# A hybrid encoder layer on one core: the first head group's inverse roots reach all partitions through memory in place of through the PE

## The chip, the cores and the metric

The kernel runs on one core of one Trainium2 chip. The metric is device time in microseconds (us) for one execution; the figure before the change is the median of three runs. Five engines run side by side, each in the order of its own queue: PE (matrix products and transposes), DVE (vector), ACT (scalar functions and copies), POOL, and SP, which here only issues transfers (DMAs). They wait for each other through semaphores. Results of PE land in PSUM, everything else that is worked on lies in on-chip memory with 128 partitions; "memory" below is the chip's DRAM.

## The reference, cut to what matters

One encoder layer over 1024 tokens of 1024 features. One projection feeds two token mixers: group A (windowed attention, 8 heads of 64) and group B (neighbourhood attention on a grid, 8 heads of 64). Each group's output, 512 features wide, is normalised by itself before the two go through one output projection. Then come a gated MLP with a convolution and a last normalisation.

```python
def rmsnorm(x, g):
    xf = x.astype(jnp.float32)
    y = xf * lax.rsqrt(jnp.mean(xf * xf, axis=-1, keepdims=True) + EPS)
    return (y * g.astype(jnp.float32)).astype(x.dtype)
...
        o_a = window_gqa_sink(qa, ka, va, sink[l])
        o_b = neighbourhood_attention(qb, kb, vb, rpb[l])
        mix = jnp.concatenate([rmsnorm(o_a, norm_a[l]), rmsnorm(o_b, norm_b[l])], axis=-1)
        h = h + jnp.einsum('bse,ed->bsd', mix, w_out[l])
...
```

The change concerns `rmsnorm(o_a, norm_a[l])` alone: for each of the 1024 tokens one number, 1/sqrt(mean square + eps), by which the 512 features of group A are multiplied.

## The kernel before

**Layout.** Activations lie transposed: features on the partitions, tokens along a row. Group A's output is four tiles `mix[0]` to `mix[3]`, each 128 features by 1024 tokens. The sum of squares over features is thus a sum over partitions and tiles, and the number that comes out for each token is needed on all 128 partitions, since every feature is multiplied by it.

**Stages.** The attention stage runs from about 50 us (its first scores start at 53.6) to about 350 us (its last product with the values at 348.5). In it two streams are interleaved: attention units (scores, softmax, transposes of the weights, products with the values) and, as filler between them, blocks of projection products (`rest`, L778). The filler's jobs are the projections of 15 column tiles (`Project`, jobs 0 to 14) and the output projection's group A part (`OutA`, jobs 15 to 22). A job has 16 steps, eight to each half of the tokens, of three matmuls each. A table `aux` hangs single pieces of work on a step: `aux[12, 5]` runs after step 5 of job 12. After the attention come the output projection and the MLP, in which PE works on one long row of products.

**What sets the order.** PE's instructions stand in the order in which the code issues them (`manual_schedule`, L136). DVE, ACT, POOL and SP are ordered by a scheduler from that stream; `tc.high_priority` (L827) lets a piece of work stand earlier than its place. Every engine then works strictly in its order: an instruction whose inputs are not there holds all that stand behind it on that engine.

**Group A's norm.** Five pieces hang in `aux` (L835). `square_a` squares and adds the four tiles to one tile `norm["sq"]` of 128 by 1024, four adds to a half. `narrow_a`, called for each half, transposes that tile in blocks of 128 tokens into PSUM and lets DVE sum each row; the second call takes the square root (ACT) and the reciprocal (DVE) of all eight columns at once. `norm["v"]` then holds, on partition p and in column c, the inverse root of token 128c + p. `wide_a(h)` spreads four columns: `widen` (L231) transposes each column, broadcast to 128 by 128, against the identity, so that all 128 output partitions get the row of 128 tokens; ACT copies the bank of 512 tokens to one half of the tile `rstda`. `wide_a(0)` hangs on step 11 and `wide_a(1)` on step 13 of job 12. The eight products `normed_a` (L831), one to a tile and half on DVE, hang on job 13; job 14, the last projection, splits the normalised tiles into two parts for the output projection.

**Beside it** on the same engines: DVE subtracts the rounded part of each block of transposed attention weights (`pl`, L430), without which PE's second product with the values (L541) cannot run; it adds the bias to the scores and takes the row minimum (L415); it takes scores of the next job's projection out of PSUM (L246). SP loads the projection's weights (`raw`, L163) and rearranges queries and keys between partitions (L304 to L307). It also loads a strip of biases for each of group B's heads (`rr`, L485): 128 rows of 489 numbers, one to a partition, that overlap and lie within 961 numbers of memory (the rows of a 16 by 8 pattern with steps of 31 and 1).

Of the kernel before, what the change touches and what calls it, by code (L numbers as in the profile page):

```python
# [13 lines left out]
F32 = mybir.dt.float32  # L14
F32R = mybir.dt.float32r
AF = mybir.ActivationFunctionType
# [3 lines left out]
D, S, HD = 1024, 1024, 64  # L20
# [37 lines left out]
def hybrid_layer(tc, xT, w_first, w_in, w_out, w_gate, w_up, w_down, small, sink, rpb, consts, rope, out):  # L58
    nc = tc.nc
    with ExitStack() as ctx:  # L60
# [7 lines left out]
        tpool = inner("temps", 3)  # L68
        apool = inner("att", 2)
        spool = inner("stats", 6)  # L70

        slots = {"xg": 16, "op": 14, "mix": 8, "rstd": 1}

        def big(name, tag, dt=F32):
            return lpool.tile([128, S], dt, name=name, tag=tag, bufs=slots[tag])
# [4 lines left out]
        def bank(name, tag):  # L80
            return psum.tile([128, HALF], F32, name=name, tag=tag)

        f32 = lambda ap: ap.bitcast(F32)
        tsl = lambda h: slice(h * HALF, (h + 1) * HALF)
# [48 lines left out]
        ident = cst[:, K_ID:K_ID + 128]  # L133
# [76 lines left out]
        def inverse_narrow(sqs, dim, tag, n=4):  # L210

            ps = bank("ss", tag)
            v = cpool.tile([128, n], F32, name="v4", tag="v4", bufs=4, padded_shape=[128, 4])
            if len(sqs) == 1:
                for c in range(n):
                    nc.tensor.transpose(ps[:, c * 128:(c + 1) * 128], sqs[0][:, c * 128:(c + 1) * 128], ident)
                with tc.high_priority(offset=500):
                    nc.vector.tensor_reduce(v, ps[:, 0:n * 128].rearrange("p (c w) -> p c w", w=128), axis=mybir.AxisListType.X, op=ALU.add)
                    nc.scalar.activation(v, v, AF.Sqrt, bias=eps, scale=1.0 / dim)
            else:  # L220
                for i, sq in enumerate(sqs):
                    for c in range(n):
                        nc.tensor.matmul(ps[:, c:c + 1], sq[:, c * 128:(c + 1) * 128], ones[:, 0:1], start=c == 0 and i == 0,
                                         stop=i == len(sqs) - 1, skip_group_check=True)
                with tc.high_priority(offset=500):
                    nc.scalar.activation(v[:, 0:n], ps[:, 0:n], AF.Sqrt, bias=eps, scale=float(D) / dim)
            with tc.high_priority(offset=500):
                nc.vector.reciprocal(v[:, 0:n], v[:, 0:n])
            return v

        def widen(v, tag, n=4):  # L231

            wide = bank("sw", tag)
            for c in range(n):
                nc.tensor.transpose(wide[:, c * 128:(c + 1) * 128], v[:, c:c + 1].to_broadcast([128, 128]), ident)
            return wide
# [327 lines left out]
        mg, h1, norm = [None] * 8, [None] * KT, {"halves": 0}  # L564
# [187 lines left out]
        live = {"op": 0}  # L752
# [23 lines left out]
        aux = {}  # L776
# [42 lines left out]
                if h == 1:  # L819
                    inverse_root(norm["v"], 512)  # L820

        def wide_a(h):
            def go():
                if h == 0:
                    live["op"] += 1
                    norm["a"] = big("rstda", "op")
                with tc.high_priority(offset=500):  # L827
                    nc.scalar.activation(norm["a"][:, tsl(h)], widen(norm["v"][:, 4 * h:4 * h + 4], "pj"), AF.Copy)
            return go

        def normed_a(i, h):  # L831
            return lambda: nc.vector.scalar_tensor_tensor(
                mix[i][:, tsl(h)], mix[i][:, tsl(h)], col(C_NA + i), norm["a"][:, tsl(h)], op0=ALU.mult, op1=ALU.mult)

        aux[11, 8], aux[12, 2], aux[12, 5], aux[12, 11], aux[12, 13] = square_a, narrow_a, narrow_a, wide_a(0), wide_a(1)  # L835
        for i in range(8):
            aux[13, 1 + i + i // 2] = normed_a(*divmod(i, 2))
        filler = rest()
# [241 lines left out]
        for h in range(2):  # L1080
            for d in range(KT):
                if h == 0 and d + 2 < KT:
                    wo.append(load_wo(d + 2, False))
                ps = bank("pj", ("o", "s", "pj")[(h * KT + d) % 3])
# [4 lines left out]
                if h == 1 and d == 1:  # L1089
                    v = inverse_narrow([total[0]], D, "pt")  # L1090
# [157 lines left out]
        v = inverse_narrow([total[1]], D, "pt")  # L1248
# [196 lines left out]
        sq, todo, vs = {}, [], {}  # L1445
# [59 lines left out]
        for i, (p, j, c) in enumerate(order):  # L1505
# [10 lines left out]
            ps = banks[p, j]  # L1516
# [26 lines left out]
        for k, cols in enumerate(quarters):  # L1543
            for j in (2, 3):
                ps = banks[6, j]
# [111 lines left out]
```

## Time and profile before

| | |
|---|---|
| median of 3 runs | 1020.83 us (1020.73 to 1021.33) |
| the profiled execution's own time | 1020.98 us |
| its span, first to last instruction | 1019.2 us |
| instructions | 14884 |
| busy: DVE | 834.7 us (82%) |
| busy: ACT | 561.6 us (55%) |
| busy: POOL | 108.6 us (11%) |
| granted clock of PE, mean | 0.998 |

The profiled execution is one more run of the kernel; times of single instructions come from it, counted from the start of its span. Work outside the span, 1.8 us of its own time, is not in the trace. Busy time is a share of the span; a matmul's end is modelled and matmuls overlap, so the start of one and the start of the next tell its price better than its length does. In a row of the timeline stand the start, the time to the end, the engine, the source line, the operation, what is written and read, and how many instructions were put together; in brackets how long the engine had been idle before and what ended that.

### The profile page before, as it was taken

What the parts mean: (1) busy time and instruction counts of PE and PEld (TensorE: products, weight loads), DVE (VectorE), ACT (ScalarE), POOL (GpSimd) and SP (SyncE); (2) the same over time, 40 slices, a digit from 0 to 9 for tenths busy, and PEclk for the clock granted to TensorE, in tenths of its full rate; (3) what the DMA queues carried; (4) which work ended last, traced back from release to release, by engine and by line L of the source; (5) the groups of instructions that cost most, each with busy time, mean ns of one, the idle gap of its engine ahead of it and who ended that gap; (6) DMA issues with size and microseconds to landing.
All of it is one profiled execution on the core that took longest, in us unless ns stands there. A gap on an engine that the chain in (4) does not pass through costs nothing.

```text
span 1019.2 us, 14884 instructions
## 1 busy us (share of the span) xinstructions
PE 1008.2 (99%) x5094; PEld 889.9 (87%) x5094; DVE 834.7 (82%) x1570; ACT 561.6 (55%) x1081; POOL 108.6 (11%) x188
## 2 busy tenths in 40 slices
PE   9999999999999999999999999999999999999996
PEld 8888888999988888888888888888888888888886
DVE  7889888768898799999987786786777688986675
ACT  8567776657676554565544443444443645544451
POOL 0233333222252100000000000000000000000002
PEclk9999999999999999999999999999999999999999
DMA  8223122333335356222552333323232698866644
GB/s 293 78 78 94 32 72 63 83 83 83 83 87 161 101 179 237 84 87 79 186 180 99 114 114 114 104 94 118 100 132 82 231 343 317 299 226 235 221 156 166
DMA packets 68220, 144.94 MB, mean 142 GB/s; under 512 B 8240, under 2 KB 18736, under 8 KB 68144
## 3 DMA queue, kind: packets, MB, share of 16 engines
q1 hardware_dynamic: 58064, 118.82, 36.0%
q10 hardware_dynamic: 10080, 25.17, 6.4%
q8 instruction: 40, 0.66, 0.3%
q14 instruction: 36, 0.29, 0.1%
HBM read 103.58 MB, written 28.57 MB: 130 GB/s over the span
## 4 chain that ended last, share of the span: by engine, by line
PE 88%; DVE 5%; ACT 3%; issue 2%; DMA 1%; DVEq 0%; SPq 0%; ACTq 0%
PE x L1017 7%; PE x L1018 7%; PE x L1016 7%; PE dn L1018 7%; PE dn L1017 7%; PE dn L1016 7%; PE pj L178 6%; PE pj L180 6%; PE pj L179 6%; PE y L1017 4%; PE y L1018 4%; PE y L1016 4%; PE s L392 3%; PE z L1017 2%; PE z L1016 2%; PE z L1018 2%
## 5 line engine op out<-in xcount | busy, mean ns | idle before, releaser
L1016 PE MATMUL x<-hg,whi 128*128 128x512 f32 x352 | 133.5, 379 | 0.0
L1017 PE MATMUL x<-hg,whi 128*128 128x512 f32 x352 | 133.4, 379 | 0.0
L1018 PE MATMUL x<-hg,wlo 128*128 128x512 f32 x352 | 133.4, 379 | 0.0
L1016 PE MATMUL dn<-xd,whi 128*128 128x512 f32 (+1 forms) x330 | 120.8, 366 | 0.0
L1018 PE MATMUL dn<-xd,wlo 128*128 128x512 f32 (+1 forms) x330 | 120.6, 365 | 0.0
L1017 PE MATMUL dn<-xd,whi 128*128 128x512 f32 (+1 forms) x330 | 120.5, 365 | 0.0
L419 ACT ACTIVATE p<-p,nm 128x385 f32<-128x385 f32 (+3 forms) x128 | 75.0, 586 | 62.5 <-DVE nm L415 59.8
L990 ACT ACTIVATE whi<-ws 128x512 fp32r<-128x512 f32 (+1 forms) x100 | 60.7, 621 | 73.8 <-DVE ws L1126 14.7
L423 POOL TENSOR_SCALAR p<-p,sm 128x384 f32<-128x384 f32 (+1 forms) x128 | 79.8, 637 | 192.0 <-DVE sm L421 159.7
L178 PE MATMUL pj<-xgh,whi 128*128 128x512 f32 x245 | 99.7, 407 | 0.0
L179 PE MATMUL pj<-xgl,whi 128*128 128x512 f32 x245 | 93.0, 379 | 0.2 <-DVE xgl L654 0.2
L180 PE MATMUL pj<-xgh,wlo 128*128 128x512 f32 x245 | 92.9, 379 | 0.0
L990 ACT ACTIVATE whi<-raw 128x512 fp32r<-128x512 f32 (+1 forms) x102 | 60.9, 610 | 48.9 <-PE x L1017 17.3
L991 DVE TENSOR_TENSOR wlo<-ws,whi 128x512 fp32r<-128x512 f32 (+1 forms) x100 | 66.5, 679 | 19.1 <-ACT whi L990 18.8
L1477 POOL TENSOR_TENSOR h<-h,wide 128x256 f32<-128x256 f32 (+1 forms) x6 | 5.4, 916 | 670.3 <-ACT wide L1473 670.3
L430 DVE TENSOR_TENSOR pl<-pt,ph 128x384 fp32r<-128x384 f32 (+2 forms) x108 | 63.6, 589 | 15.6 <-ACT ph L429 13.7
L1016 PEld LDWEIGHTS x<-hg,whi 128*128 128x128 f32 x352 | 66.5, 189 | 9.5
L1018 PEld LDWEIGHTS x<-hg,wlo 128*128 128x128 f32 x352 | 66.5, 189 | 9.5
L1017 PEld LDWEIGHTS x<-hg,whi 128*128 128x128 f32 x352 | 66.5, 189 | 9.4
L991 DVE TENSOR_TENSOR wlo<-raw,whi 128x512 fp32r<-128x512 f32 (+1 forms) x102 | 66.5, 668 | 5.1 <-ACT whi L990 5.1
L1018 PEld LDWEIGHTS dn<-xd,wlo 128*128 128x128 f32 x330 | 62.5, 189 | 8.1 <-DVE wlo L991 0.4
L1347 ACT ACTIVATE xd<-xd 128x512 fp32r<-128x512 f32 x77 | 47.3, 625 | 40.2 <-DMA xd<-x 39.7
(267 smaller groups left out, 2515.2 us busy)
## 6 DMA issues: line engine op xcount, KB each, us to landing
xd<-x SPq DMA_DIRECT2D x77, 256.0 KB, 5.1
raw<-in_w_down_dram SPq DMA_DIRECT2D x72, 256.0 KB, 4.5
raw<-in_w_gate_dram SPq DMA_DIRECT2D x22, 512.0 KB, 3.4
raw<-in_w_up_dram SPq DMA_DIRECT2D x22, 512.0 KB, 3.5
x<-c ACTq DMA_DIRECT2D x22, 512.0 KB, 2.6
raw<-in_w_in_dram SPq DMA_DIRECT2D x30, 256.0 KB, 2.8
raw<-in_w_down_dram SPq DMA_DIRECT2D x36, 192.0 KB, 4.4
x<-t ACTq DMA_DIRECT2D x11, 512.0 KB, 2.6
```

The costliest lines, as they stand in the source:

```text
L178: nc.tensor.matmul(ps, w[0], mv(x[0][:, tsl(h)]), start=first, stop=False)
L179: nc.tensor.matmul(ps, w[0], mv(x[1][:, tsl(h)]), start=False, stop=False)
L180: nc.tensor.matmul(ps, w[1], mv(x[0][:, tsl(h)]), start=False, stop=last)
L419: nc.scalar.activation(p[:, j, 0:e], p[:, j, 0:e], AF.Exp, bias=nm, scale=-1.0, accum_out=sm[:, j:j + 1])
L423: nc.gpsimd.tensor_scalar(p[:, i, 0:m], p[:, i, 0:m], sm[:, i:i + 1], 1.0, op0=ALU.mult, op1=ALU.mult)
L430: mark["rest"] = nc.vector.tensor_tensor(pl[:, 0:n], ps[:, 0:n], f32(ph[:, 0:n]), op=ALU.subtract)
L990: nc.scalar.activation(hi, src, AF.Copy)
L991: nc.vector.tensor_tensor(lo, src, f32(hi[:, :, :]), op=ALU.subtract)
L1016: nc.tensor.matmul(ps, w[0], x[0], start=first and i == 0, stop=False, skip_group_check=True)
L1017: nc.tensor.matmul(ps, w[0], x[1], start=False, stop=False, skip_group_check=True)
L1018: nc.tensor.matmul(ps, w[1], x[0], start=False, stop=last and i == len(ws) - 1, skip_group_check=True)
L1347: nc.scalar.activation(hi, f32(lo), AF.Copy)
```

## The change

In place of `wide_a(0)` and `wide_a(1)` one piece, `wide_a`, hangs on step 9 of job 12. One transpose turns the 128 by 8 tile of inverse roots into 8 rows of 128 tokens in a PSUM bank. ACT copies them to the first eight partitions of `norm["sq"]`, whose sums of squares are no longer needed. SP writes the eight rows to a buffer `roots` in memory, 4 KB, and then reads that buffer, 1024 tokens in a row, once for each of the 128 partitions into the tile `rstda`. The eight products on DVE are the same and read the same tile; where they stand in DVE's order is set by the scheduler.

```diff
+        spread_pool = ctx.enter_context(tc.tile_pool(name="roots", bufs=1, space=bass.MemoryType.DRAM))
+        roots = spread_pool.tile([8, 128], F32, name="roots")
...
-        def wide_a(h):
-            def go():
-                if h == 0:
-                    live["op"] += 1
-                    norm["a"] = big("rstda", "op")
-                with tc.high_priority(offset=500):
-                    nc.scalar.activation(norm["a"][:, tsl(h)], widen(norm["v"][:, 4 * h:4 * h + 4], "pj"), AF.Copy)
-            return go
+        def wide_a():
+            live["op"] += 1
+            norm["a"] = big("rstda", "op")
+            ps, row = bank("row", "pj"), norm["sq"][0:8, 0:128]
+            nc.tensor.transpose(ps[0:8, 0:128], norm["v"], ident)
+            with tc.high_priority(offset=500):
+                nc.scalar.activation(row, ps[0:8, 0:128], AF.Copy)
+                nc.sync.dma_start(roots, row)
+                nc.sync.dma_start(norm["a"], bass.AP(tensor=roots.tensor, offset=roots.offset, ap=[[0, 128], [1, S]]))
...
-        aux[11, 8], aux[12, 2], aux[12, 5], aux[12, 11], aux[12, 13] = square_a, narrow_a, narrow_a, wide_a(0), wide_a(1)
+        aux[11, 8], aux[12, 2], aux[12, 5], aux[12, 9] = square_a, narrow_a, narrow_a, wide_a
```

Source lines of the changed kernel lie two to three higher. Three places of the engines' orders show what moves.

**SP, from the rearranging of one head's queries and keys on.** Before:

```order
L305 DMA q<-kb 64x1024
L307 DMA ka<-kb 64x1024
L306 DMA kb<-ka 64x1024
L163 DMA raw<-in_w_in_dram 128x512
L163 DMA raw<-in_w_out_dram 128x512
L485 DMA rr<-in_rpb_dram 128x1x489
```

and now:

```order
L307 DMA q<-kb 64x1024
L309 DMA ka<-kb 64x1024
L308 DMA kb<-ka 64x1024
L831 DMA roots<-sq 8x128
L165 DMA raw<-in_w_in_dram 128x512
L832 DMA rstda<-roots 128x1024
L165 DMA raw<-in_w_out_dram 128x512
L487 DMA rr<-in_rpb_dram 128x1x489
```

The write of the eight rows stands directly behind the last rearranging transfer, the read for all partitions one weight load later; the load of the output projection's first weights stands behind both.

**DVE, while job 12 ends.** `mixa` is group A's output, `rstda` the spread roots. Before, five of the eight products stood here:

```order
L430 TENSOR_TENSOR pl<-pt,ph 128x384
L832 TENSOR_SCALAR mixa<-mixa,par,rstda 128x512
L415 ISA p,nm<-s,xb 128x384
L415 ISA nm 128x1
L832 TENSOR_SCALAR mixa<-mixa,par,rstda 128x512 x4
L430 TENSOR_TENSOR pl<-pt,ph 128x384
L246 TENSOR_TENSOR t<-pj,rstd_334 128x8x8x8
```

and now none does:

```order
L432 TENSOR_TENSOR pl<-pt,ph 128x384
L417 ISA p,nm<-s,xb 128x384
L417 ISA nm 128x1
L432 TENSOR_TENSOR pl<-pt,ph 128x384
L248 TENSOR_TENSOR t<-pj,rstd_337 128x8x8x8
```

The five have gone further down; everything else keeps its place among itself.

**DVE, some ten instructions later, in job 13.** `v` are the values of a later pair of heads. Before, three products stood ahead of the second `pl` of 256 columns, and that `pl` stood ahead of the copy of job 13's first half out of PSUM (L246):

```order
L421 RECIPROCAL sm<-sm 128x2
L832 TENSOR_SCALAR mixa<-mixa,par,rstda 128x512
L430 TENSOR_TENSOR pl<-pt,ph 128x384
L415 ISA p,nm<-s,xb 128x384
L415 ISA nm 128x1
L832 TENSOR_SCALAR mixa<-mixa,par,rstda 128x512 x2
L334 TENSOR_TENSOR v<-vt,v 128x4x64
L430 TENSOR_TENSOR pl<-pt,ph 128x256
L334 TENSOR_TENSOR v<-vt,v 128x4x64
```

and now, from the same reciprocal on:

```order
L423 RECIPROCAL sm<-sm 128x2
L835 TENSOR_SCALAR mixa<-mixa,par,rstda 128x512
L432 TENSOR_TENSOR pl<-pt,ph 128x384
L417 ISA p,nm<-s,xb 128x384
L417 ISA nm 128x1
L835 TENSOR_SCALAR mixa<-mixa,par,rstda 128x512 x2
L336 TENSOR_TENSOR v<-vt,v 128x4x64
L835 TENSOR_SCALAR mixa<-mixa,par,rstda 128x512
L336 TENSOR_TENSOR v<-vt,v 128x4x64
L432 TENSOR_TENSOR pl<-pt,ph 128x256
```

The next rows, of which the first two are as before and the others in another order, were

```order
L415 ISA p,nm<-s,xb 128x384
L415 ISA nm 128x1
L421 RECIPROCAL sm<-sm 128x2
L430 TENSOR_TENSOR pl<-pt,ph 128x256
L246 TENSOR_TENSOR t<-pj,rstd_334 128x8x8x8
```

and now are

```order
L417 ISA p,nm<-s,xb 128x384
L417 ISA nm 128x1
L835 TENSOR_SCALAR mixa<-mixa,par,rstda 128x512 x2
L248 TENSOR_TENSOR t<-pj,rstd_337 128x8x8x8
L432 TENSOR_TENSOR pl<-pt,ph 128x256
L423 RECIPROCAL sm<-sm 128x2
```

So the first of the eight products, the first instruction of DVE that needs the read from memory, stands behind the reciprocal where the sixth stood before, and six products stand ahead of the second `pl` of 256 columns; the last two follow later, singly.

## The prediction

> **What bounds the kernel now.** I read the page first: the busy shares and the chain of work that ended last.
>
> ```profile
> PE 1008.2 (99%) x5094; PEld 889.9 (87%) x5094; DVE 834.7 (82%) x1570; ACT 561.6 (55%) x1081; POOL 108.6 (11%) x188
> ...
> PE 88%; DVE 5%; ACT 3%; issue 2%; DMA 1%; DVEq 0%; SPq 0%; ACTq 0%
> ```
>
> PE is busy for 99% of the span, and the chain runs through PE for 88%. The second view is what PE waited for, over the whole run.
>
> ```profile
> PE warm_ps L147 <- POOL eps L142: 1.0, 1, 1.0
> PE o L541 <- DVE pl L430: 1.0, 2, 0.7
> PE sw L235 <- DVE v L228: 1.0, 2, 0.6
> PE ss L223 <- ACT s L1495: 0.6, 1, 0.6
> PE s L392 <- DVE nm L415: 0.2, 1, 0.2
> PE pj L179 <- DVE xgl L654: 0.2, 1, 0.2
> ```
>
> Eight waits, 4.0 us in all. Two kinds concern the attention stage: a product with the values that waits for `pl` (1.0 us) and scores that wait for their bank (0.2). The third view is the stretch of the change, by engine.
>
> ```profile
> core 0: us, PE busy (x) PEld busy (x) DVE busy (x) ACT busy (x) POOL busy (x), PEclk, DMA share, GB/s
> ...
> 266.00:274.00 8.00, 8.00 (x49) 7.19 (x48) 7.91 (x16) 4.25 (x10) 1.50 (x2) 1.00 0.36 101
> 274.00:282.00 8.00, 8.00 (x52) 7.33 (x51) 6.41 (x20) 5.17 (x16) 2.34 (x4) 1.00 0.00 0
> ```
>
> PE is busy 8.00 of 8.00 us. So a microsecond that PE is spared there is a microsecond of the kernel, one that PE has to wait is one more, and there is nothing later in which a delay would be swallowed, since later waits are so few. DVE is at 7.91 in the first stretch and 6.41 in the second: it is nearly full, which matters below.
>
> **What PE is spared.** The chain of waits, limited to this stretch, prices the two spreads (start, time, what).
>
> ```profile
> 263.10 0.44 PE sw L235 x4
> ...
> 265.55 0.46 PE sw L235 x4
> ```
>
> Eight transposes go: 0.44 + 0.46 = 0.90 us. One comes: eight rows out, but still 128 columns, so a quarter of 0.44 as the upper bound and nothing as the lower; I take 0.11. PE's sum is -0.79 us, and this is all that the change can give to the bound engine directly.
>
> **What ACT is spared.** Two copies go, a small one comes.
>
> ```profile
> L828 ACT ACTIVATE rstda<-sw x2: 578/582/585, 263.8 to 266.6; 128x512 f32<-128x512 f32 x2
> ```
>
> That is 1.16 us less the copy of 8 by 128, which costs 0 to 0.58. ACT had 3.75 us of 8 idle here (4.25 busy, above), so I book nothing.
>
> **The way through memory.** The roots themselves are ready when they were. What follows is SP's order: the write stands behind the last rearranging transfer (`kb<-ka`), the read behind one weight load and behind the landing of the write.
>
> ```profile
> 264.88 0.46 SPq L306 DMA_DIRECT2D kb<-ka  x1
> 265.45 0.52 SPq L163 DMA_DIRECT2D raw<-in_w_in_dram  x1
> 270.74 0.33 SPq L163 DMA_DIRECT2D raw<-in_w_out_dram  x1
> ```
>
> The eight rows are in place by then: PE's transpose now stands ahead of where the first spread stood (263.10, above), and the copy behind it is shorter than the old one of 0.58. So the write is issued where the weight load was, at 265.45, the load half a microsecond later, and then SP stands until the write has landed. What is queued behind on SP is the weight load that was issued at 270.74; SP is free again well before that, so nothing else comes late from SP. The prices of transfers, from issue to landing:
>
> ```profile
> raw<-in_w_gate_dram SPq DMA_DIRECT2D x22, 512.0 KB, 3.4
> ...
> raw<-in_w_in_dram SPq DMA_DIRECT2D x30, 256.0 KB, 2.8
> ...
> xr<-in_xT_dram SPq DMA_DIRECT2D x8, 512.0 KB, 5.6
> h1d<-h ACTq DMA_DIRECT2D x16, 256.0 KB, 3.7
> ...
> kb<-ka SPq DMA_DIRECT2D x9, 256.0 KB, 2.9
> ...
> rr<-in_rpb_dram SPq DMA_DIRECT2D x8, 244.5 KB, 3.7
> out_dram<-h SPq DMA_DIRECT2D x13, 128.0 KB, 1.7
> ```
>
> The write is 4 KB to memory. Nearest rows: 1.7 us for 128 KB (`out_dram`) as the lower bound, 3.7 for 256 KB (`h1d`) as the upper: landed at 267.15 to 269.15. Ahead of it on the same queue runs `kb<-ka`, issued at 264.88, which lands after 2.9 at 267.78; I take 267.9. SP needs some 0.05 more, so the read is issued at 267.95 (267.2 to 269.2).
>
> The read is 512 KB, 128 rows of 4 KB. A weight load of that size takes 3.4; `xr`, of exactly this shape on this queue, 5.6: these are the bounds. What the trace has of many partitions reading one small piece of memory is `rr`: 128 rows that overlap, all drawn from 961 numbers or 3.8 KB. Its 244.5 KB take 3.7 where a plain 256 KB load takes 2.8: 0.9 more, and for twice the bytes 1.8 more, which makes 3.4 + 1.8 = 5.2. Two of three rows lie at the upper end, so I take 5.4. Landed: T = 267.95 + 5.4 = 273.35, with 270.6 (267.2 + 3.4) and 274.8 (269.2 + 5.6) as its ends.
>
> The Trainium skill, page "DMA: Bandwidth & Descriptors", section "Anatomy of one DMA — SWDGE (gpsimd) path", gives a transfer a fixed 2.0 us, mostly the receipt of the last byte, and then its bytes at 436 GB/s (a fit for POOL's path, not SP's); it warns that a write to memory can take surprisingly long to be confirmed. By it the pair would take 2.0 + 3.2 = 5.2 us, an estimate that lands at 270.65. For 512 KB it agrees with the weight loads (3.2 against 3.4) and disagrees with `xr` (5.6).
>
> **Who waits.** DVE's rows around the products, as they ran:
>
> ```profile
> 264.39 1.05 DVE L832 SCALAR_TENSOR_TENSOR mixa<-mixa,par,rstda 128x512 f32<-128x512 f32 x1
> ...
> 265.85 2.73 DVE L832 SCALAR_TENSOR_TENSOR mixa<-mixa,par,rstda 128x512 f32<-128x512 f32 x4
> 268.50 0.54 DVE L430 TENSOR_TENSOR pl<-pt,ph 128x384 fp32r<-128x384 f32 x1
> ...
> 271.62 0.17 DVE L421 RECIPROCAL sm<-sm 128x2 f32<-128x2 f32 x1
> 271.70 0.73 DVE L832 SCALAR_TENSOR_TENSOR mixa<-mixa,par,rstda 128x512 f32<-128x512 f32 x1
> 272.46 0.56 DVE L430 TENSOR_TENSOR pl<-pt,ph 128x384 fp32r<-128x384 f32 x1
> 272.94 0.55 DVE L415 CUSTOM_DVE_ANT_0 p<-s,xb 128x384 f32<-128x384 f32 x1
> ...
> 273.41 1.41 DVE L832 SCALAR_TENSOR_TENSOR mixa<-mixa,par,rstda 128x512 f32<-128x512 f32 x2
> 274.74 0.41 DVE L334 TENSOR_TENSOR v<-vt,v 128x256 fp32r<-128x256 f32 x1
> ...
> 275.60 0.42 DVE L334 TENSOR_TENSOR v<-vt,v 128x256 fp32r<-128x256 f32 x1
> 275.94 0.55 DVE L415 CUSTOM_DVE_ANT_0 p<-s,xb 128x384 f32<-128x384 f32 x1
> ...
> 277.54 0.42 DVE L430 TENSOR_TENSOR pl<-pt,ph 128x256 fp32r<-128x256 f32 x1
> 277.88 0.68 DVE L246 TENSOR_TENSOR t<-pj,rstd 128x512 f32<-128x512 f32 x1
> 278.48 0.55 DVE L415 CUSTOM_DVE_ANT_0 p<-s,xb 128x384 f32<-128x384 f32 x1
> ```
>
> Five products go from 264.39 to 268.50, worth 265.37 - 264.39 = 0.98 and 268.50 - 265.85 = 2.65. DVE then reaches the reciprocal (271.62) earlier, but not by 3.63, because its scores, copies and `pl` in between wait for PE, which is only 0.79 ahead: the row behind the five starts on what PE ended just before. I take 1.6, so the first product's turn comes at about 270.1 (between 268.1, all of it, and 271.7, none); this matters only if T lies before it. It then stands there until T, and holds everything behind it: `pl`, two score rows, the value rows, the copy out of PSUM, and the reciprocal that POOL waits for.
>
> From the moment it runs, DVE works without a gap in the new order, in start-to-start prices of these rows: product 0.76 (271.70 to 272.46), `pl` 0.48, scores 0.47, two products 1.33 (273.41 to 274.74), `v` 0.33, a product 0.67, `v` 0.34, `pl` of 256 columns 0.34, scores 0.48, two products 1.33, the copy out of PSUM 0.60 (277.88 to 278.48), and the second `pl` of 256 columns until its end, 0.42. The sum is 7.55, and with 0.05 for the semaphore PE's product on that `pl` can start at T + 7.6. That product, and the one on the `pl` before it, ran here:
>
> ```profile
> 277.02 0.28 PE L541 MATMUL o<-pl,v 128*128 128x256 f32 x1
> ...
> 278.44 0.28 PE L541 MATMUL o<-pl,v 128*128 128x256 f32 x1
> ```
>
> So the kernel's end moves by T + 7.6 - 278.44 = T - 270.84. The `pl` before is done 4.72 + 0.05 after T and is needed at 277.02, which is T - 272.25: weaker by 1.4. The later rows of DVE, counted in the same way, ask for less. The change costs nothing only if T is before 270.84, and gives all of its 0.79 if T is before 270.05.
>
> Two more edits cost nothing: the tile `norm["sq"]` is held until the write has read it, by about 268, and the next copy into a tile of its pool is that at 277.88, or 9.9 us of cover; the products themselves are read much later, in job 14.
>
> **The sum.** T = 273.35 gives +2.51, with PE's 0.79 in it already (the unstalled PE would be at 277.65). On the profiled execution's 1020.98 us that is 1023.5; this execution lies 0.15 over the median of the three runs, so against these 1023.3.
>
> **The rivals.**
>
> *The read comes back fast.* If it runs like the weight loads, T is 270.6 to 272.3 and the kernel moves by -0.2 to +1.4: 1020.6 to 1022.2. For it: the weight loads, most of the kernel's transfers of these sizes, run at 2.8 and 3.4, and `xr`'s 5.6 may hold time behind other transfers of its queue, which the row does not tell. Against it: `rr`, the one row with a shared source, is the slow one of its size. The Trainium skill's fit, above, would put it at this case's fast end: 270.65, or -0.2.
>
> *The read is hidden altogether,* the case on the other side: it lands before DVE gets to the first product, at 270.1, and PE keeps the whole 0.79: 1020.0. It decides at T = 270.05. Against it: both lower bounds together give 270.6.
>
> *It gets faster by more.* The five products leave DVE's fullest stretch (7.91 of 8), and PE's waits for `pl` and for scores vanish with it. Price: 0.79 and at most the 1.2 us of these two rows, 1018.8. Against it: PE did not wait once in these 16 us.
>
> *The shared source is slow,* all 128 rows being drawn from one 4 KB piece one behind the other: at twice `rr`'s surcharge the read takes 7.0 or more, T = 275, +4.1 or more: 1025 and up. Against it: `rr` draws its rows from 3.8 KB, no larger a piece, and pays 0.9.
>
> **How the numbers follow.** Chances: the forecast (T from 272.3 to 274.8, +1.4 to +4.0) 0.58, the fast read 0.27, hidden altogether 0.06, faster by more 0.04, the slow source 0.05. What a measurement of this kernel can tell from no change is about 0.2%, 2.04 us. Of the forecast's case about 0.10 lies under +2.04. So slower is 0.48 + 0.05 = 0.53, faster 0.04, the same 0.43. The likeliest case alone is 1022.2 to 1024.8; the range for 8 in 10 takes in most of the fast read and a little of the slow source: 1020.5 to 1025.0.
>
> **What would show it.** Right: in the changed profile DVE idles just before the first product, released by the read; the read's landing row shows 5 us or so; PE waits once or twice for `pl` at L543, 2 to 4 us in all, where it had waited not at all; the two `sw` groups of the chain are gone and a single `row` of about 0.1 us has come. The step on the write is wrong if SP's read is issued outside 267.2 to 269.2. The step on the read is wrong if it lands in 3.4. The step on DVE is wrong if PE waits for another tile than `pl`, or more or less than T - 270.05 of them. The prediction as a whole is wrong if no wait of PE is left near 278: then the time is 1020.0.

## The result and the profile after

The changed kernel takes 1022.86 us, the median of 22 runs (1021.37 to 1024.7), against 1021.2 us for the kernel before in 22 runs on the same chip (1019.81 to 1022.03). The ratio is 1.0017, with a 95% interval of 1.0011 to 1.0023: it is 1.7 us slower, between 1.1 and 2.3. The profiled execution took 1023.0 us, its span is 1021.2 (1019.2 before).

The page's busy times and the shares of the chain that ended last:

```profile
PE 1008.5 (99%) x5087; PEld 889.8 (87%) x5087; DVE 834.2 (82%) x1570; ACT 560.7 (55%) x1080; POOL 108.9 (11%) x188
...
PE 85%; DVE 7%; ACT 4%; issue 2%; DMA 1%; POOL 0%; DVEq 0%; ACTq 0%; POOLq 0%
```

PE's busy time is the old one within 0.3 us, but 2.0 us more of span go by; DVE's share of the chain grew from 5% to 7%. What PE waited for (engine, line, releaser: us in all, times, longest):

```profile
PE o L543 <- DVE pl L432: 1.8, 4, 0.7
PE sw L237 <- DVE v L230: 1.3, 2, 0.7
PE warm_ps L149 <- POOL eps L144: 1.0, 1, 1.0
PE pj L180 <- DVE v L336: 0.9, 1, 0.9
PE ss L225 <- ACT s L1498: 0.6, 1, 0.6
PE s L394 <- DVE nm L417: 0.2, 1, 0.2
```

Two entries answer for the change: the products that wait for `pl` went from 1.0 us in two waits to 1.8 in four, and a wait is new that the prediction had not named, a projection matmul (`pj`) for `v`, 0.9. The wait for `v` and 0.55 of the waits for `pl` stand in one stretch; the fourth entry, 0.23 at 295.20, lies behind it, where the same product had idled 0.13 before. The same view of stretches as before:

```profile
core 0: us, PE busy (x) PEld busy (x) DVE busy (x) ACT busy (x) POOL busy (x), PEclk, DMA share, GB/s
...
266.00:274.00 8.00, 8.00 (x48) 7.27 (x47) 5.21 (x12) 2.94 (x7) 1.15 (x2) 1.00 0.59 167
274.00:282.00 8.00, 6.55 (x39) 5.58 (x39) 7.94 (x20) 4.43 (x13) 1.27 (x3) 1.00 0.00 0
```

PE, 8.00 of 8.00 before, is at 6.55 in the second stretch, and the load on DVE has swapped: 5.21 where it was 7.91, 7.94 where it was 6.41. The chain of waits limited to 264 to 282 us tells why (start, time, what):

```profile
265.53 2.43 DMA roots<-sq
...
267.98 4.00 DMA rstda<-roots
...
272.00 0.76 DVE mixa L835
272.79 0.56 DVE pl L432
...
276.06 0.24 DVE v L336
...
276.39 0.41 DVE pl L432
...
278.52 0.45 DVE t L248
...
279.12 0.42 DVE pl L432
...
279.59 0.38 PE o L543
```

The write takes 2.43 us, the read 4.00, and from 272.00 on one DVE row follows the other to the `pl` of 279.12, on which PE's product of 279.59 waits. That product ran at 278.44 before. DVE stood idle in front of the first product, and PE in front of two matmuls:

```profile
270.04 0.17 DVE L423 RECIPROCAL sm<-sm 128x2 f32<-128x2 f32 x1
272.00 0.75 DVE L835 SCALAR_TENSOR_TENSOR mixa<-mixa,par,rstda 128x512 f32<-128x512 f32 x1 [1.79 <-DMA rstda<-roots]
```

```profile
260.69 0.27 PE L828 MATMUL row<-cst,v 128*8 128x128 f32 x1
...
276.62 0.45 PE L180 MATMUL pj<-xgh,whi 128*128 128x512 f32 x1 [0.89 <-DVE v L336]
...
279.59 0.38 PE L543 MATMUL o<-pl,v 128*128 128x256 f32 x1 [0.55 <-DVE pl L432]
...
295.20 0.38 PE L543 MATMUL o<-pl,v 128*128 128x256 f32 x1 [0.23 <-DVE pl L432]
```

Idle time understates the loss. PE idled 0.89 + 0.55 = 1.44 in the stretch, but it came 0.78 earlier than in the old profile and left 1.17 later, which is 1.95 (the next section says how this is counted). Its matmuls overlap: in these rows one of 0.38 is followed by the next start after 0.21 or 0.22, and the view counts a wait only from the modelled end of the matmul before.

### The profile page after: what moved, and what is told of

The parts are those of the page before. It is cut to its first block, busy times and chain, and to the rows that moved or that the text cites. A ratio compares the mean times of both kernels' runs of the same rounds, so it can differ in the third digit from the quotient of the medians.

```text
span 1021.2 us, 14873 instructions
## 1 busy us (share of the span) xinstructions
PE 1008.5 (99%) x5087; PEld 889.8 (87%) x5087; DVE 834.2 (82%) x1570; ACT 560.7 (55%) x1080; POOL 108.9 (11%) x188
## 4 chain that ended last, share of the span: by engine, by line
PE 85%; DVE 7%; ACT 4%; issue 2%; DMA 1%; POOL 0%; DVEq 0%; ACTq 0%; POOLq 0%
PE x L1019 7%; PE x L1020 7%; PE x L1021 7%; PE dn L1021 6%; PE dn L1019 6%; PE dn L1020 6%; PE pj L180 6%; PE pj L182 6%; PE pj L181 6%; PE y L1020 4%; PE y L1019 4%; PE y L1021 4%; PE s L394 2%; PE z L1019 2%; PE z L1021 2%
## 5 line engine op out<-in xcount | busy, mean ns | idle before, releaser
L180 PE MATMUL pj<-xgh,whi 128*128 128x512 f32 x245 | 99.7, 407 | 0.9 <-DVE v L336 0.9
L432 DVE TENSOR_TENSOR pl<-pt,ph 128x384 fp32r<-128x384 f32 (+2 forms) x108 | 63.5, 588 | 16.8 <-ACT ph L431 14.8
L1020 PEld LDWEIGHTS dn<-xd,whi 128*128 128x128 f32 x330 | 62.5, 189 | 7.7
## 6 DMA issues: line engine op xcount, KB each, us to landing
xd<-x SPq DMA_DIRECT2D x77, 256.0 KB, 5.0
raw<-in_w_down_dram SPq DMA_DIRECT2D x72, 256.0 KB, 4.4
raw<-in_w_in_dram SPq DMA_DIRECT2D x30, 256.0 KB, 2.8
```

What stands on the lines that cost most here:

```text
L180: nc.tensor.matmul(ps, w[0], mv(x[0][:, tsl(h)]), start=first, stop=False)
L432: mark["rest"] = nc.vector.tensor_tensor(pl[:, 0:n], ps[:, 0:n], f32(ph[:, 0:n]), op=ALU.subtract)
L1020: nc.tensor.matmul(ps, w[0], x[1], start=False, stop=False, skip_group_check=True)
```

## The experiments

**How they are read.** PE runs the same matmuls in the same order in all these kernels, but for the eight transposes and the one. So the start of each PE instruction can be compared with the start of the same one in the first profile of the kernel before. The *net* of the stretch is the median of that difference between 279 and 287 us, less the median between 244 and 260 us, which is ahead of the change's place. T is the start of DVE's first product, which the read releases but for the last two rows of the table below, where DVE came to it no earlier than the data. The prediction's formula is T - 270.84, with T put into the old kernel's clock (less the shift of PE at 244 to 260 us). Where the text says when the parts of a transfer had landed, it goes by the semaphore updates in the trace, 16 for each of these reads and loads.

Three theories went in. A: the loss is the time at which the read lands, through DVE's order. B: it is the new order of DVE's rows, products close together ahead of `pl`, whatever T is. C: it is the added traffic and the round trip as such.

**The write on ACT's queue.**

```diff
-                nc.sync.dma_start(roots, row)
+                nc.scalar.dma_start(roots, row)
```

> The write of the eight rows is issued by ACT, so SP's read no longer stands behind the weight load; DVE's rows keep the order of the changed kernel. Theory A (the loss is the time at which the read lands, T, through DVE, and the stretch moves by T - 270.84, at least -0.79): T falls from 272.0 to about 269.5, DVE does not idle in front of the first product, PE's two waits (for v, 0.89, and for pl, 0.55) go, the stretch is -0.6 to -0.8 against the kernel before, and the time 1020.4 to 1020.7 where that kernel takes 1021.2. Theory B (the loss is DVE's new order, with the products close together ahead of pl): T does not matter, the waits for v and pl stay within 0.3 us, +1.1 to +1.7. Theory C (the loss is the added traffic of 512 KB and a round trip, wherever the products are): +1.1 to +1.7, and the lost time shows at PE's waits for something other than v or pl.

1021.73 us, ratio 1.0004 (0.9995 to 1.0013). SP's read now stands directly behind `kb<-ka`. ACT had issued the write at 261.75, and it had landed at 265.02, 3.27 us later, just as SP came to the read:

```profile
264.46 0.46 SPq L308 DMA_DIRECT2D kb<-ka  x1
265.04 0.51 SPq L832 DMA_DIRECT2D rstda<-roots  x1
265.64 0.54 SPq L165 DMA_DIRECT2D raw<-in_w_in_dram  x1
```

```profile
rstda<-roots SPq DMA_DIRECT2D x1, 512.0 KB, 5.0
```

The read itself took 5.0 us rather than 4.0. A 256 KB weight load was issued 0.6 us behind it and `kb<-ka` 0.6 ahead, but that these are the reason is not shown: 15 of its 16 parts had landed after 4.06, the last after 4.98. So T is 270.04 and not 269.5. PE lists no wait for `v` any more and none for `pl` in the stretch (the third one of this profile, 0.2, is at 293.26); the net is -0.40, where -0.6 to -0.8 was expected. The order of DVE's products is that of the changed kernel and the traffic too, so B and C both fall for the stretch. The whole, +0.44, missed the expected 1020.4 to 1020.7; its interval, -0.5 to +1.3, holds the net too. What the profile lost elsewhere is taken up below.

**The read in two halves.**

```diff
-                nc.sync.dma_start(norm["a"], bass.AP(tensor=roots.tensor, offset=roots.offset, ap=[[0, 128], [1, S]]))
+                for t in range(2):
+                    nc.sync.dma_start(norm["a"][:, tsl(t)], bass.AP(tensor=roots.tensor, offset=roots.offset + t * HALF, ap=[[0, 128], [1, HALF]]))
...
-            aux[13, 1 + i + i // 2] = normed_a(*divmod(i, 2))
+            aux[13, 1 + i + i // 2] = normed_a(i % 4, i // 4)
```

> The read comes as two of 256 KB, and the four products of the first half of the tokens come first; DVE's rows keep their order otherwise. Theory A: the first half lands at about 271.0 to 271.2 in place of 272.0, and the stretch is +0.2 to +0.4 against the kernel before instead of +1.1. Theory B: the order on DVE is the same, so +1.1 as in the changed kernel. Theory C: the same bytes, so +1.1 or, for one more transfer, a little more.

1022.66 us, ratio 1.0013 (1.0004 to 1.0022). Half the bytes did not come in half the time (the other half was issued 0.38 us behind), and the write was slower here:

```profile
265.13 2.87 DMA roots<-sq
...
268.01 3.37 DMA rstda<-roots
```

T is 271.40, later than expected; the formula gives +0.66 for it, and the net is +0.75. By itself this run separates little; with the others it is one more point on the line.

**One hop more.**

```diff
-                nc.sync.dma_start(norm["a"], bass.AP(tensor=roots.tensor, offset=roots.offset, ap=[[0, 128], [1, S]]))
+                nc.sync.dma_start(again, roots)
+                nc.sync.dma_start(norm["a"], bass.AP(tensor=again.tensor, offset=again.offset, ap=[[0, 128], [1, S]]))
```

> The eight rows are copied once more from memory to memory before they are read, which makes T later by some 2.2 to 2.5 us (a write of 4 KB took 2.45 in the changed kernel), so 274.2 to 274.5. DVE has one product fewer between T and the second pl of 256 columns (5 products, by its order of instructions), 0.67 us less. Theory A: the stretch moves by T - 271.5, which is +2.7 to +3.0, the total +3.2 to +3.6 over the kernel before. Theory B: one product fewer ahead of pl, so no more than the changed kernel's +1.1 to +1.7. Theory C: 4 KB more of traffic, so as the changed kernel, +1.7.

1025.14 us, ratio 1.0038 (1.0025 to 1.0050), so +3.85; net +2.70, where B and C had at most +1.7.

```profile
268.00 2.11 DMA again<-roots
270.12 3.85 DMA rstda<-again
```

```profile
275.40 0.43 PE L543 MATMUL o<-pl,v 128*128 128x384 f32 x1 [0.98 <-DVE pl L432]
...
278.95 0.45 PE L180 MATMUL pj<-xgh,whi 128*128 128x512 f32 x1 [1.93 <-DVE v L336]
```

T is 2.0 later than in the changed kernel, the net 1.5 more and the timed runs 2.2 more, with a product fewer ahead of the second `pl` of 256 columns. But PE did not wait for that `pl` here. It waited for `v`, whose matmul starts 4.95 after T in this order and ran at 276.26 before, so that it asks for T - 271.31, which is +2.62. The expected T - 271.5 gives +2.43 and came near by another tile than it named.

**The products held back in DVE's order.**

```diff
-            return lambda: nc.vector.scalar_tensor_tensor(
-                mix[i][:, tsl(h)], mix[i][:, tsl(h)], col(C_NA + i), norm["a"][:, tsl(h)], op0=ALU.mult, op1=ALU.mult)
+            def go():
+                with behind("rest"):
+                    nc.vector.scalar_tensor_tensor(
+                        mix[i][:, tsl(h)], mix[i][:, tsl(h)], col(C_NA + i), norm["a"][:, tsl(h)], op0=ALU.mult, op1=ALU.mult)
+            return go
...
-            aux[13, 1 + i + i // 2] = normed_a(*divmod(i, 2))
+            aux[13, 3 + i + i // 2] = normed_a(*divmod(i, 2))
```

> The read is as in the changed kernel (T near 272.0), but the eight products are held back in DVE's order, so that at most one stands ahead of each pl. Theory A as extended to a chosen order: the first product's turn on DVE comes at 271 to 272, so DVE hardly idles, the second pl of 256 columns is in time, and the stretch is -0.6 to -0.8, the total 1020.4 to 1020.7 where the kernel before takes 1021.2. Theory B (order) says the same here, which is why this run tells only C from the two: Theory C keeps +1.1 to +1.7, since the transfers are those of the changed kernel.

1021.92 us, ratio 1.0008 (0.9999 to 1.0017). ```profile
272.13 0.75 DVE L837 SCALAR_TENSOR_TENSOR mixa<-mixa,par,rstda 128x512 f32<-128x512 f32 x1 [1.41 <-DMA rstda<-roots]
```

T is 272.13, as late as in the changed kernel, yet the net is +0.16 and not +1.2: with two products ahead of the second `pl` of 256 columns in place of six, the late read finds less behind it. Theory C falls again, and T alone is not the whole of A: it is T plus what stands between the first product and the row that PE needs. The expected -0.6 did not come, for DVE still idled 1.41 for the read, and PE idled 0.2 for `v` at 275.85 and again for `pl` at 280.57. By 319 us PE was 1.2 us later still: it waited there for `pl` (0.81 at 302.43) and for copies out of PSUM (L248), with products pushed into these stretches.

**Both kernels profiled once more**, unchanged.

> The changed kernel, profiled once more. T and the stretch are set by the order: T again 272.0 within 0.15, PE's waits for v (0.89) and pl (0.55) again, and the stretch +1.1 within 0.15. The landing of the load near 350 took 3.98 after its issue; if it varies from run to run, it differs here by more than 0.2, and if the change sets it, it is 4.0 again.

It gave the cleanest test, by chance. The program is the same to the last instruction, and the read took 4.85 us where it had taken 4.00:

```profile
265.48 2.50 DMA roots<-sq
...
267.99 4.85 DMA rstda<-roots
```

```profile
277.48 0.46 PE L180 MATMUL pj<-xgh,whi 128*128 128x512 f32 x1 [1.59 <-DVE v L336]
280.44 0.38 PE L543 MATMUL o<-pl,v 128*128 128x256 f32 x1 [0.55 <-DVE pl L432]
```

T is 272.86, the formula +2.22, the net +2.31. Theory A holds for the stretch, and the claim that T is set by the order does not: it varies by 0.9 us between two executions. More than half of that is one late part: 15 of the read's 16 parts had landed after 4.02 us here and after 3.76 in the first profile, the last after 4.85 and 4.00. Why it was late is open.

> The kernel before, profiled once more, to see how far PE's wait for v near 356 (0.32 us in its first profile, 0.67 in the changed kernel, 1.20 with the write on ACT) varies by itself. That wait follows ACT's wait for the second load of w_out that SP issues near 350. If the landing of that load varies from run to run: ACT's row on it starts 3.5 to 4.6 us after SP's issue here as well, and differs from the 3.64 of the first profile by up to 0.9. If the change makes it later: 3.6 again, within 0.1.

The kernel before, a second time: 1022.02 us. The stretch moved by 0.06, but at 356 us it lost 1.0 us against its own first profile. The chain of waits there, in the first profile and in the second:

```profile
350.14 3.01 DMA raw<-in_w_out_dram
...
355.96 0.62 PE sw L235 x4
```

```profile
350.45 4.03 DMA raw<-in_w_out_dram
...
357.30 0.62 PE sw L235 x4
```

A load of `w_out` took 3.01 us in the one and 4.03 in the other, and PE's transposes behind it were later by 1.3, of which this profile had been 0.3 late before. Over the twelve profiles it took 2.87 to 4.06, with and without the change. The ten profiles of changed kernels lost between -0.1 and 1.0 there, 0.4 on average, the two of the kernel before 0 and 1.0. So what the changed kernel lost there (0.34), and the write on ACT (0.88), lies within what the kernel before shows by itself.

**A source of 128 different rows**, twice.

```diff
-        roots = spread_pool.tile([8, 128], F32, name="roots")
+        roots = spread_pool.tile([128, S], F32, name="roots")
...
-                nc.sync.dma_start(roots, row)
-                nc.sync.dma_start(norm["a"], bass.AP(tensor=roots.tensor, offset=roots.offset, ap=[[0, 128], [1, S]]))
+                nc.sync.dma_start(roots[0:1].rearrange("a (c w) -> (a c) w", w=128), row)
+                nc.sync.dma_start(norm["a"], roots)
...
+        aux[8, 4] = lambda: nc.sync.dma_start(roots, xT[0])
```

> The read takes 128 different rows of memory instead of one row 128 times; the other rows hold input data copied there early, so the roots are wrong for every partition but the first. DVE's order is that of the changed kernel. If the shared source costs something (0.6 of the 4.0 us measured, over the 3.4 of a 512 KB weight load): the read takes 3.4, T falls to 271.4, and the stretch moves by T - 270.84 = +0.6. If it costs nothing: 4.0 as in the changed kernel, T near 272.0, +1.1.

> The read of 128 different rows once more (it took 3.2 us from SP's issue to DVE's first product, where the shared row took 4.0, 4.3 and 4.9 in three profiles of the same order). The roots are again wrong for every partition but the first. If the shared source costs something: 3.2 again, within 0.3, and T near 271.2. If the difference was chance: 4.0 to 4.9.

```profile
265.46 2.43 DMA roots<-sq
...
267.91 3.20 DMA rstda<-roots
```

```profile
267.95 3.20 DMA rstda<-roots
```

3.20 us both times, in the same queue and the same place, where the one shared row of 4 KB took 4.00, 4.27 and 4.85 (and 3.85 behind the second hop). In these two runs 127 of the 128 rows hold other data than the roots; nothing else of the read was changed. So the shared source costs 0.7 to 1.7 us. Without the last of the 16 parts it is 0.6 to 0.9 (3.76 to 4.05 in the changed kernel, its second profile and the products held back, against 3.14 and 3.16). That different rows never vary is not shown by two runs: a 256 KB weight load issued in the changed kernel at 266.06 had one late part as well, 3.87 where the other 15 had landed after 2.95. T is 271.13 and 271.18, the nets +0.52 and +0.50. The times, single runs of 1022.68 and 1022.88, hold a load of `w_out` at 356 us of 3.62 and 4.06.

**Both cures together**: the write on ACT and the products held back. The edit is that of the first experiment and that of the fourth.

> The write on ACT's queue (T near 270.0) and the products held back, both together. Theory A for the stretch: T - 270.84 is at its floor, -0.8 where the write on ACT alone gave -0.4 to -0.5. What the order of the held products lost in the run before (1.0 us where PE waits for pl near 302) is a matter of order and not of T, so it is expected again: the whole is +0.2 to +0.6, no better than the write on ACT alone. If that loss came from T, it goes, and the whole is -0.4 to -0.8, faster than both kernels.

1021.58 us against 1021.52, ratio 1.0001 (0.9992 to 1.0010). The net is -0.73, all that PE is spared. Then 1.0 is lost between 300 and 306 us, as with the products held back alone (0.9): some 0.6 at one wait, which was 0.26 in the kernel before, and the rest where a projection waits for a copy out of PSUM, 0.18 at 304.45. The larger one:

```profile
300.50 0.43 PE L543 MATMUL o<-pl,v 128*128 128x384 f32 x1 [0.87 <-DVE pl L432]
```

**Held back, but early.** As above, with the products on the steps of the changed kernel.

```diff
-            aux[13, 3 + i + i // 2] = normed_a(*divmod(i, 2))
+            aux[13, 1 + i + i // 2] = normed_a(*divmod(i, 2))
```

> The write on ACT's queue (T near 270.0) and the products behind pl in DVE's order, but in the places of the changed kernel, so that the last of them ends before 284 and the rows from 285 on stand in nearly the old order. Theory A with order as a cause of its own: the stretch is at its floor of -0.8 as in the run before, and the 1.0 that was lost near 301 there shrinks to the 0.3 that the changed kernel loses between 287 and 296: the whole is -0.4 to -0.6, 1020.9 to 1021.1 where the kernel before takes 1021.5. If the loss near 301 comes back (a wait of PE for pl of 0.7 or more), order is not what made it, and the whole is 0 as with the products held longer.

1021.5 us against 1021.38, ratio 1.0000 (0.9991 to 1.0009). PE's waits over the whole profile are now nearly those of the kernel before:

```profile
PE warm_ps L149 <- POOL eps L144: 1.0, 1, 1.0
PE o L543 <- DVE pl L432: 1.0, 2, 0.7
PE sw L237 <- DVE v L230: 0.8, 2, 0.6
PE ss L225 <- ACT s L1501: 0.6, 1, 0.6
PE s L394 <- DVE nm L417: 0.2, 1, 0.2
```

The net is -0.73, the loss at 301 is gone, and 0.38 is lost between 287 and 296. Less its shift, the profile ends 0.5 us ahead of the old kernel, as expected. The timed runs did not come out at the expected 1020.9 to 1021.1, and their interval, -0.9 to +0.9, cannot tell -0.5 from nothing. No kernel here is shown to be faster than the one before.

**All points of the stretch** (us; "shift" is how much later PE was at 244 to 260 us than in the old profile, "floor" the least that T can make of it, the 0.79 that PE is spared):

| kernel | T | shift | formula | net measured |
|---|---|---|---|---|
| changed | 272.00 | +0.08 | +1.08 | +1.17 |
| changed, again | 272.86 | -0.20 | +2.22 | +2.31 |
| write on ACT | 270.04 | -0.32 | -0.48 | -0.40 |
| two halves | 271.40 | -0.10 | +0.66 | +0.75 |
| 128 different rows | 271.13 | -0.01 | +0.30 | +0.52 |
| the same, again | 271.18 | +0.02 | +0.32 | +0.50 |
| one hop more (T - 271.31, by `v`) | 274.00 | +0.07 | +2.62 | +2.70 |
| products held back | 272.13 | -0.05 | none, other order | +0.16 |
| write on ACT, held | 270.08 | -0.61 | floor, -0.79 | -0.73 |
| write on ACT, held early | 270.38 | -0.27 | floor, -0.79 | -0.73 |

The first six have the same order of rows on DVE, but for one row of a weight load where ACT writes. T moves by 2.7 us over them in the old kernel's clock, and the net by 2.7.

## Why the prediction was right, and where it was off

**Direction and mechanism: right.** The read-back holds DVE in front of the first product, and DVE's gapless rows hand the delay to PE. The forecast was +2.5 us and 1023.3; measured are +1.7 and 1022.86. The 1023.3 counts from the median of three runs; from the 1021.2 of 22 it would read 1023.7. The text put what can be told from no change at 2.04 us. With 22 runs of each kernel 1.7 is told from nothing, so the 0.43 for "the same" hung on too wide a limit.

**What PE is spared: right.** -0.79 was forecast; in ten profiles of changed kernels PE is 0.72 to 0.78 ahead once the two spreads are past.

**The write: right.** SP's read was to be issued at 267.95 and was issued at 267.98, with 267.84 to 268.01 in all the other kernels that keep the write on SP. The write itself took 2.43 from its issue, where the forecast had 2.4 because `kb<-ka` runs ahead of it. The changed profile fits that reason, limited to 264 to 268 us:

```profile
kb<-ka SPq DMA_DIRECT2D x1, 256.0 KB, 2.9
```

`kb<-ka` landed at 267.87 and the write at 267.96, and in six of the seven profiles with the write on SP it came 0.08 to 0.12 behind (0.45 in that of the two halves). That `kb<-ka` held it is not shown: on ACT's queue the write took 3.04 to 3.27 with no transfer of that queue ahead of it, and the second hop, with a weight load of SP's queue still in flight, 2.11.

**The read: the term that was mis-sized.** 5.4 us was booked, with 3.4 and 5.6 as ends; it took 4.00 and 4.85 in the two profiles. The step that failed is "Two of three rows lie at the upper end, so I take 5.4". The surcharge for a shared source, 1.8, was the right kind of term: 0.7 to 1.7 by the runs with different rows. But it was put on 3.4, where a read of this size in this place takes 3.20. And the upper end, 5.6, is no median of eight loads. The view tells the landing of one `xr` alone in the profile before:

```profile
DMA to landing us min/median/max: 5.6/5.6/5.6
```

It is the slowest of the eight: by the semaphore updates in the same trace they took 3.41 to 5.62, half of them under 4.5. So only one of the three rows, `rr`, spoke for the upper end, and by itself it gave 5.2. The weight loads were no more typical: beside the 30 loads of 256 KB at 2.8 the same page has 72 of `w_down` at 4.5 and 77 of `xd` at 5.1, so that "most of the kernel's transfers of these sizes, run at 2.8 and 3.4" is not so.

The Trainium skill, page "DMA: Bandwidth & Descriptors", section "Anatomy of one DMA — SWDGE (gpsimd) path", has a fit for POOL's path of 2.0 us plus the bytes at 436 GB/s, for 512 KB an estimate of 3.2 us. On SP's queue the different rows agree (3.20), and the shared row does not (4.00 and 4.85).

**When DVE comes to the first product: right.** 270.1 was forecast; its reciprocal ran at 270.04 and it then idled 1.79.

**T - 270.84: right.** +1.08 against +1.17, and over the five other profiles of that order within 0.22. PE was said to wait T - 270.05 in all, which is 1.87 for T = 271.92 in the old clock; it lost 1.95 (1.17 plus the 0.78 that it had gained).

**Which tile PE waits for: half wrong.** The text made `pl` the only one. In the stretch PE idled 0.55 for `pl`, where 2 to 4 had been named as the sign, and before that 0.89 for `v` at 276.62: this `pj` goes into the bank that DVE's row on `vt` reads, and that row stands behind the fourth product. The matmul starts 4.62 after T and ran at 276.26 before, so it asks for T - 271.64, 0.8 less than the `pl` behind it, and cost nothing of its own: PE lost at 276.62 what it would have lost at 279.59. A wait that is passed on the way to a stronger one changes the list of waits and not the sum. With one hop more it was the stronger one, as shown above.

**"The later rows of DVE ask for less": off by 0.3.** Every profile with the changed kernel's order on DVE loses 0.29 to 0.36 more between 287 and 296 us; the wait of 0.23 for `pl` at 295.20 is part of it. It is much the same for a T of 270.04 and one of 272.86 (0.35 and 0.29), so it goes with the order and not with T: behind the stretch theory B has this much of the truth. What makes that `pl` late was not taken apart.

**The sum of the profiled execution:** +1.17 in the stretch, +0.33 behind it, +0.34 by the load at 356 us that varies by itself, +0.1 in the rest, together 1.9 of the 2.0 by which the spans differ; the remaining 0.1 is the shift ahead of the change.

**The rivals.** The fast read came half true: T = 272.0 lies inside the rival's 270.6 to 272.3, and 272.86 in the forecast's own case. The border, for which the text gives no sum, ran through what one kernel does from execution to execution. That the whole, +1.7, lies in the forecast's +1.4 to +4.0 is in part luck: in the first profile the stretch alone, +1.17, belongs to the fast read, and the loss behind it, 0.3, which the text put at nothing, makes up for a part of the read that was booked too long. Hidden altogether did not happen; it takes a write that is issued earlier as well as fewer products ahead of `pl`, and is then worth -0.73. Faster by more and the slow source (7.0 or more) did not occur.

## What to carry to other kernels

Price a detour through memory as two latencies, here 2.4 to 3.3 us for 4 KB out and 3.9 to 5.2 for one row read back to 128 partitions, look at how many transfers the price that you take rests on, and then look at which engine's order the result stands in: an idle DVE row costs the microseconds that the engine behind it has no slack for. The price is T plus the rows between the waiting instruction and the one that the bound engine needs, so either a landing that comes earlier or moving those rows away cures it; the second took back 1.0 of 1.2 us here, until the rows stood in the way of a later stretch. Issue the write on a queue that is free when the data is there: on SP it stood behind other transfers until 265.53 and landed at 267.96, on ACT it went at 261.75 and landed at 265.02.

## What the runs showed of the hardware

- 128 partitions reading one 4 KB row took 3.85 to 4.85 us for 512 KB, and 128 different rows 3.20 in the same place, twice. With 256 KB transfers issued 0.6 us ahead of it and behind it on the queue the shared row took 5.0 to 5.2 (three kernels); that they are the reason is not shown, for with such a load 0.4 us behind it the row took 3.85, and once 4.85 with none issued within 0.9 us of it.
- The same transfer of the same program varies: 4.00 and 4.85 for the read, 3.01 and 4.03 for a 256 KB load of weights (2.87 to 4.06 over all twelve profiles). That one load moves the kernel's end by up to 1.0 us from execution to execution, as much as the effect under study; a difference of two single profiles in that range says nothing until its place is known.
- Halving a read from 512 to 256 KB took it only from 4.0 or more to 3.37 us, with the other half issued 0.38 us behind.
- The 4 KB write took 2.43 to 2.50 us on SP's queue (2.87 once) and 3.04 to 3.27 on ACT's, three profiles.
